# More buffers in the scan, one tile moved, and a replayed instruction order in a two-layer hybrid diffusion step

## The chip, the cores and the metric

One Trainium2 chip, all 8 NeuronCores (two dies of four). Each core runs the same program on its own 1536 tokens, and the metric is device time in microseconds (us) of the slowest core. Some executions fall in a slow state, in which one die (once both) has a lower granted clock and the time is up to 18% longer; those are left out of every ratio. Ratios are the mean time of one kernel's fast runs over the mean of the fast runs of the kernel before in the same rounds on the same chip. The medians that are quoted beside them are those of all runs, slow ones too, so the ratios are not quite the ratios of the medians. A difference of two ratios is turned into time with 2232 us, and then compares kernels that ran in different rounds.

## The reference, cut to what matters

```python
def trunk_layer(x, mods, l, P, init_state, rows):           # twice (DEPTH = 2)
    sh1, sc1, g1, sh2, sc2, g2 = mods
    y, st = token_mixer(x * (1 + sc1) + sh1, l, P, init_state, rows)
    x = layer_norm(ALPHA * x + g1 * y, ...)
    y = swiglu(x * (1 + sc2) + sh2, P['w_gate_up'][l], P['w_down'][l])
    return layer_norm(ALPHA * x + g2 * y, ...), st

def token_mixer(u, l, P, init_state, rows):
    z = u @ P['w_in'][l] + P['b_in'][l]                      # q, k, v, o, gates, Fourier, conv, merge gates
    h, new_state = mlstm_bidir(...)                          # 4 heads of 256, chunks of 128, two directions
    ...                                                      # Fourier mixing, gated short convolution
    merged = sigmoid(gm) * (h_m @ ...) + sigmoid(gf) * (h_f @ ...) + sigmoid(gc) * (h_c @ ...)
    return merged @ P['w_out'][l], new_state
```

The scan (`mlstm_bidir`) goes over chunks in order in both directions. It starts from a cached state C0 for the sample tokens and from zero for the context tokens, and the state after every second chunk is an output.

## The kernel before

The kernel does not write instructions in order. It records operations with their data dependences, and a list scheduler with assumed costs then puts them in an order for each of the five engines. At run time each engine takes its own row strictly in that order and waits on semaphores. In the lines of the profile PE is TensorE, DVE VectorE, ACT ScalarE, POOL GpSimd and SP SyncE, which issues transfers. Buffers are places in SBUF: two tiles that share a place make a dependence between whatever uses them.

The assumed cost of a transfer, in the scheduler:

```python
            if o.kind == "dma":
                s = max(dma_t, t + 1300.0)
                dma_t = s + o.nbytes / dma_rate              # dma_rate = 300 bytes per ns
                o.t1 = dma_t + 700.0
```

The buffers of the scan (kT: keys of a head; ktok: the same, transposed back to tokens; C: states, stored to oC and loaded from C0n; Cb: their bf16 copies; sc: scores; h and hn: outputs of the scan before and after their normalisation):

```python
        kT = R.sb("kT%d" % l, [128, 2, NTOK], BF16, v_p[1].end + 6144)
        ktok = R.sb("ktok%d" % l, [128, NCH, 256], BF16, SG + 4096)
        C_p = Pool(R, "C%d" % l, bv_p.end, [128, 2, 257], F32, 5)
        s_p = Pool(R, "sc%d" % l, ht_p1.end, [128, 512], BF16, 3)
```

One head of the scan:

```python
            for g in range(3):                    # scores and transposed keys, 4 chunks a group
                ...
            for k in range(4):                    # context chunks 8 to 11, both directions
                ...                               # each step: vw on GpSimd, state update on PE, DVE, ACT
            Cc = []
            for d in range(2):
                t = C_p.get()                     # a free state buffer
                R.dma("sp", t[:]..., C0n[l, d, h], ...)
                Cc.append(t)
            for k in range(8):                    # sample chunks 0 to 7, both directions
                ...
        def proj_o(l, h):
            for b in range(3):                    # output gate of the head, by blocks of 512 tokens
                for ec in range(2):
                    pt = proj(oW, ec * 128, 128, b)
                    so = so_p.nxt()
                    R.act(so[:], pt(), AF.Sigmoid, ...)
                    d = hm[h][:, ec, b * 512:(b + 1) * 512]
                    R.tt(d, d, so[:], ALU.mult, n=512, cost=431)
```

The merge stage works with weight tiles r and partial sums ac and mo. It folds Fourier weights (wf) from a staging tile (wst) that lies over buffers of the convolution, and brings x back from memory; in layer 0 GpSimd adds position rows to one block of x:

```python
        ws_p = Pool(R, "wst%d" % l, X + 16 * K1, [128, 4, 2, 128], F32, 1)
        wf_p = Pool(R, "wf%d" % l, ws_p.end, [128, 8, 128], BF16, 2)
        ...
    R.schedule(allowed)
    R.emit_all()
```

## Time and profile before

| | before |
|---|---|
| median of 16 runs, 3 of them slow | 2234.7 us (4 runs when the prediction was made, 1 of them slow: 2235.02) |
| spans of the cores in the profiled run | 2214.7 to 2232.7 us, granted clock 0.987 to 0.992 |
| TensorE (PE) busy, core 6 | 2108.9 us, 94% |
| without a matmul | 123.8 us |

TensorE sets the time, so the profile is read by asking where it stands still. The stages are cut at events: the first state update of a layer begins its scan, the first product of the layer's input u with an r tile ends it, the first product with mg ends the merge, the first gate_up product ends the norm. Length, and the time in it without a matmul, in us, from the timeline and the windows of the slowest core:

| stage | length | idle |
|---|---|---|
| start | 115.5 | 46.8 |
| scan, layer 0 | 255.3 | 24.9 |
| conv and merge, layer 0 | 368.3 | 8.9 |
| norm, FFN and projections between the scans | 469.6 | 6.8 |
| scan, layer 1 | 250.9 | 16.8 |
| conv and merge, layer 1 | 350.7 | 2.3 |
| norm and FFN to the end | 422.5 | 17.2 |

### The profile page before, as it was taken

The page shows a single profiled execution, that of the slowest core. Times are in us where ns is not written, and L with a number is a line of the kernel's source. Part 1 is how long each engine was busy: PE and PEld are TensorE (multiplying, and loading weights), DVE is VectorE, ACT ScalarE, POOL GpSimd, SP SyncE. Part 2 cuts the span into 40 slices and gives each one's busy share as a digit, 9 for nine tenths or more (in the row PEclk, how much of TensorE's full clock was granted, in tenths as well). Part 3 has the DMA queues.
Part 4 walks back from the last instruction along what each step waited for, and adds up shares of the span by engine and source line. Part 5 has one row for each costly group of instructions (what it writes and reads, how often), then busy time and mean ns, then how long its engine had stood idle before and what let it go on. Part 6 is the DMA issues. An engine that isn't in the chain of part 4 may idle for free.

```text
span 2232.7 us, 29934 instructions; the slowest of 8 cores (2214.7 to 2232.7 us)
## 1 busy us (share of the span) xinstructions
PE 2108.9 (94%) x12092; PEld 1092.8 (49%) x12092; DVE 1153.6 (52%) x2229; ACT 872.9 (39%) x1471; POOL 607.7 (27%) x1003
## 2 busy tenths in 40 slices
PE   2898998998999999999999999899999999999997
PEld 1565674443444434444446657544444443444446
DVE  2765775554444772222576667745544469111256
ACT  1466764222222471111355777522222238111124
POOL 1443452113221440011354344311111136000022
PEclk9999999999999999999999999999999999999999
DMA  9634245566443264454035334433533236332212
GB/s 207 137 84 95 72 124 96 104 118 137 81 85 65 83 108 81 90 109 76 38 82 135 77 92 109 105 48 52 132 57 60 41 104 108 57 57 38 53 38 76
DMA packets 73625, 195.97 MB, mean 88 GB/s; under 512 B 7162, under 2 KB 34824, under 8 KB 71824
## 3 DMA queue, kind: packets, MB, share of 16 engines
q0 software_dynamic: 34688, 120.71, 31.7%
q1 hardware_dynamic: 38800, 73.36, 9.6%
q8 instruction: 95, 1.56, 0.3%
q14 instruction: 42, 0.34, 0.1%
HBM read 272.67 MB, written 39.94 MB: 140 GB/s over the span
## 4 chain that ended last, share of the span: by engine, by line
PE 83%; DMA 7%; DVE 6%; ACT 2%; POOL 1%; issue 1%; SPq 0%; DVEq 0%
PE ps L192 82%; DVE x L234 2%; DMA qW<-wpack 2%; DMA oC<-C 1%; DMA wst<-wpack 1%; PE ps L190 1%; DVE C L246 1%; DMA r<-wpack 1%; DMA C<-C0n 1%; DMA x<-xin 1%; ACT x L222 0%; DVE x L246 0%; DVE zsr L234 0%; DMA oW<-wpack 0%; DVE ac L234 0%
## 5 line engine op out<-in xcount | busy, mean ns | idle before, releaser
L192 PE MATMUL ps<-u,r 128*128 128x512 bf16 x2304 | 515.4, 379 | 1.4 <-DVE uc1b L246 0.8
L192 PE MATMUL ps<-u,gu 128*128 128x512 bf16 x2112 | 464.0, 381 | 9.1 <-DVE g L234 7.2
L192 PEld LDWEIGHTS ps<-u,r 128*128 128x128 bf16 x2304 | 222.2, 98 | 268.3 <-issue 2.7
L192 PEld LDWEIGHTS ps<-u,gu 128*128 128x128 bf16 x2112 | 205.2, 98 | 259.6 <-DVE g L234 9.1
L234 DVE TENSOR_TENSOR g<-ps,sa 128x512 bf16<-128x512 f32 x132 | 90.7, 690 | 325.2 <-PE ps L192 325.2
L192 PE MATMUL ps<-g,wd 128*128 128x512 bf16 (+1 forms) x1232 | 230.2, 349 | 0.0
L222 ACT ACTIVATE sa<-ps 128x512 f32<-128x512 f32 x132 | 78.5, 596 | 342.5 <-PE ps L192 342.4
L192 PEld LDWEIGHTS ps<-g,wd 128*128 128x128 bf16 x1232 | 119.8, 98 | 108.4 <-issue 1.0
L222 ACT ACTIVATE sg<-ps,cpk 128x512 f32<-128x512 f32 x102 | 70.0, 686 | 188.2 <-PE ps L192 175.1
L298 POOL DMA_DIRECT2D r<-wpack x112 | 63.1, 564 | 281.0 <-PE ps L192 280.8
L246 DVE SCALAR_TENSOR_TENSOR C<-C,tA__56,ps 128x514 f32<-128x514 f32 x160 | 115.9, 742 | 41.0 <-PE ps L192 33.9
L234 DVE TENSOR_TENSOR x<-x,rn 128x512 f32<-128x512 f32 (+1 forms) x202 | 135.9, 740 | 0.0
L246 DVE SCALAR_TENSOR_TENSOR x<-ps,g1a,x 128x512 f32<-128x512 f32 (+1 forms) x104 | 72.5, 703 | 110.3 <-PE ps L192 109.5
L222 ACT ACTIVATE Cb<-C,tA__56 128x514 bf16<-128x514 f32 x160 | 113.1, 721 | 31.5 <-DVE C L246 17.6
L298 POOL DMA_DIRECT2D gu<-wpack x60 | 32.3, 539 | 313.4 <-PE ps L192 309.4
L258 POOL TENSOR_SCALAR vw<-v,gat 128x257 bf16<-128x257 bf16 x192 | 97.8, 520 | 72.2 <-PE ps L192 64.2
L192 PE MATMUL ps<-u,kW 128*128 128x512 bf16 x384 | 94.6, 394 | 10.9 <-ACT u L222 8.1
L192 PE MATMUL ps<-vW,u 128*128 128x256 bf16 (+1 forms) x768 | 96.2, 277 | 0.0
L192 PE MATMUL ps<-u,oW 128*128 128x512 bf16 x384 | 93.6, 393 | 1.3 <-DMA oW<-wpack 1.1
L192 PE MATMUL ps<-u,qW 128*128 128x512 bf16 x384 | 89.4, 379 | 2.1 <-ACT q L222 1.2
L192 PE MATMUL ps<-hm,r 128*128 128x512 bf16 x384 | 90.9, 379 | 0.0
L192 PE MATMUL ps<-hc,r 128*128 128x512 bf16 x384 | 90.7, 379 | 0.0
(253 smaller groups left out, 2966.1 us busy)
## 6 DMA issues: line engine op xcount, KB each, us to landing
r<-wpack POOLq DMA_DIRECT2D x80, 512.0 KB, 6.3
gu<-wpack POOLq DMA_DIRECT2D x60, 512.0 KB, 6.7
oC<-C SPq DMA_DIRECT2D x96, 256.0 KB, 2.3
wd<-wpack POOLq DMA_DIRECT2D x16, 704.0 KB, 12.5
x<-xin SPq DMA_DIRECT2D x5, 2048.0 KB, 14.5
xspill<-x SPq DMA_DIRECT2D x4, 2048.0 KB, 6.8
r<-wpack POOLq DMA_DIRECT2D x32, 256.0 KB, 6.3
wst<-wpack SPq DMA_DIRECT2D x16, 512.0 KB, 3.8
```

Source lines behind the costliest of these rows:

```text
L190: ins = PE.transpose(out=rap(m[0]), in_=m[1], identity=m[2])
L192: ins = PE.matmul(rap(m[0]), lhsT=m[1], rhs=m[2], start=m[3], stop=m[4])
L222: ins = A.activation(out=rap(out), in_=rap(in_), func=func, **kw)
L234: ins = E.tensor_tensor(out=rap(out), in0=rap(a), in1=rap(b), op=op)
L246: ins = V.scalar_tensor_tensor(out=rap(out), in0=rap(a), scalar=rap(s), in1=rap(b), op0=op0, op1=op1)
L258: ins = E.tensor_scalar(out=rap(out), in0=rap(a), scalar1=s1, scalar2=s2, op0=op0, **kw)
L298: ins = E.dma_start(out=out, in_=in_, **kw)
```

## The change

Its intent: take away waits of TensorE in the scan and at the start of the merge, and let the order be chosen by replaying it against a finer model of the transfers. No computing instruction is added or taken away on any engine; only the number of semaphore instructions differs (29934 instructions in all before, 29916 after). The core of the diff:

```diff
-        kT = R.sb("kT%d" % l, [128, 2, NTOK], BF16, v_p[1].end + 6144)
+        kTs = [R.sb("kT%d_%d" % (l, i), [128, 2, NTOK], BF16, a) for i, a in enumerate((v_p[1].end + 6144, G + 18 * K1))]
...
-        ktok = R.sb("ktok%d" % l, [128, NCH, 256], BF16, SG + 4096)
+        ktoks = [R.sb("ktok%d_%d" % (l, i), [128, NCH, 256], BF16, a) for i, a in enumerate((SG + 4096, G + 12 * K1, SG + 4096, v_p[1].end + 6144))]
...
-        s_p = Pool(R, "sc%d" % l, ht_p1.end, [128, 512], BF16, 3)
+        s_p = Pool(R, "sc%d" % l, ht_p1.end, [128, 512], BF16, 2)
+        for i in range(2):
+            C_p.free.append(R.sb("Cx%d_%d" % (l, i), [128, 2, 257], F32, s_p.end + i * 2080))
...
-            for g in range(3):
+            for g in (2, 0, 1):
...
+            (the two C0 loads moved ahead of the four context steps)
...
-            for b in range(3):
+            for b in (2, 0, 1):                  # in proj_o
...
-        ws_p = Pool(R, "wst%d" % l, X + 16 * K1, [128, 4, 2, 128], F32, 1)
-        wf_p = Pool(R, "wf%d" % l, ws_p.end, [128, 8, 128], BF16, 2)
+        ws_p = Pool(R, "wst%d" % l, X + 28 * K1, [128, 4, 2, 128], F32, 1)
+        wf_p = Pool(R, "wf%d" % l, X + 16 * K1, [128, 8, 128], BF16, 2)
...
-    R.schedule(allowed)
+    R.settle(allowed, 6)        # schedule, replay, feed the replayed transfer times back; best of six
+    (the eight adds of position rows moved apart on GpSimd's row)
```

The v bias tile bv also moves to the front of its region, so that it can be loaded before the second block of x has been used. `settle` and `replay` are some 100 lines that only choose an order.

More of the change, by code (lines that the diff above doesn't have):

```diff
@@ L16 @@
     __slots__ = ("i", "eng", "emit", "deps", "odeps", "cost", "prio", "kind", "tiles", "acc", "nd", "succ",
-                 "est", "t0", "t1", "seqno", "vc", "xdeps", "semkey", "semval", "nbytes", "lead", "tset")
+                 "est", "t0", "t1", "seqno", "vc", "xdeps", "semkey", "semval", "nbytes", "lead", "tset", "row")
 class PT:
@@ L91, in __init__ @@
         self.outputs, self.outkeys = set(), set()
+        self.took, self.log = None, []
         self.fine = set()
@@ L303, in dma @@
         o.lead = chain
+        o.row = 1.0
         if str(out.space) == "DRAM" and out.tensor.name in self.outputs:
@@ L476, in schedule @@
             if o.kind == "dma":
-                s = max(dma_t, t + 1300.0)
-                dma_t = s + o.nbytes / dma_rate
-                o.t1 = dma_t + 700.0
+                if self.took is not None:
+                    o.t1 = t + self.took[o.i]
+                else:
+                    s = max(dma_t, t + 1300.0)
+                    dma_t = s + o.nbytes / dma_rate
+                    o.t1 = dma_t + 700.0
                 fin = o.t1
@@ L505, in schedule, with replay, moving, head @@
         return order
+    def replay(self, seed=None, rate=330.0):
+        import random
+        rng = random.Random(seed)
+        vary = (lambda a, b: rng.uniform(a, b)) if seed is not None else (lambda a, b: 1.0)
+        order = self.order
+        rate *= vary(0.9, 1.05)
+        at = {e: 0 for e in order}
+        free = {e: 0.0 for e in order}
+        end, issued, took = {}, {}, {}
+        queue = {"pool": [], "sp": []}
+        clock, tset = 0.0, None
+        left = len(self.ops)
+        waits = {o: [(d, 0.0 if d.kind == "dma" or d.eng == o.eng else LAT[d.eng]) for d in list(o.deps) + o.xdeps] for o in self.ops}
+        def moving():
+            return [q[0] for q in queue.values() if q and q[0][1] <= clock + 1e-6]
+        ready = {}
+        def head(e):
+            o = order[e][at[e]]
+            t = free[e]
+            for d, lat in waits[o]:
+                x = end.get(d)
+                if x is None:
+                    return None
+                if x + lat > t:
+                    t = x + lat
+            return t
+        while left or queue["pool"] or queue["sp"]:
+            best = None
+            for e in ENGS:
+                if at[e] < len(order[e]):
+                    t = ready.get(e)
+                    if t is None:
+                        t = ready[e] = head(e)
+                    if t is not None and (best is None or t < best[0]):
+                        best = (t, e)
+            mv = moving()
+            nxt = None
+            if mv:
+                total = sum(h[3] for h in mv)
+                nxt = clock + min(h[2] * total / (rate * h[3]) for h in mv)
+            for q in queue.values():
+                if q and q[0][1] > clock + 1e-6 and (nxt is None or q[0][1] < nxt):
+                    nxt = q[0][1]
+            if nxt is not None and (best is None or nxt <= best[0]):
+                t = nxt
+            else:
+                t = max(best[0], clock)
+            for h in mv:
+                h[2] -= (t - clock) * rate * h[3] / total
+            clock = t
+            for n, q in queue.items():
+                if q and q[0][1] <= clock + 1e-6 and q[0][2] <= 1.0:
+                    o = q.pop(0)[0]
+                    end[o] = clock + (700.0 if n == "pool" else 500.0)
+                    took[o.i] = end[o] - issued[o]
+                    if q:
+                        q[0][1] = max(q[0][1], clock)
+            if nxt is not None and (best is None or nxt <= best[0]):
+                continue
+            t, e = best
+            o = order[e][at[e]]
+            at[e] += 1
+            left -= 1
+            ready[e] = None
+            c = o.cost * (1.0 if e == "pe" else vary(0.97, 1.06))
+            if e == "act" and o.tset is not None and o.tset != tset:
+                tset = o.tset
+                c += 1300.0
+            if o.kind == "dma":
+                if e == "pool":
+                    c = 550.0
+                issued[o] = t
+                n = o.nbytes
+                queue[e].append([o, max(t + 1300.0, 4500.0) if e == "pool" else t + 900.0, n * vary(0.97, 1.06), o.row])
+            else:
+                end[o] = t + c
+            free[e] = t + c
+        return max(end.values()), took
@@ L507, in emit_all, with settle @@
+    def settle(self, allowed, tries):
+        best = None
+        for i in range(tries):
+            used = self.took
+            self.schedule(allowed)
+            t, took = self.replay()
+            mean = (t + sum(self.replay(s)[0] for s in range(3))) / 4
+            self.log.append((i, t, mean))
+            if best is None or mean < best[0]:
+                best = (mean, used)
+            self.took = took
+        self.took = best[1]
+        self.schedule(allowed)
     def emit_all(self):
@@ L885, in build_program @@
     un = {"n": 0}
+    PL = []
     def add_places(b, eng="dve", gp=0):
@@ L893, in add_places @@
             z = xb[b][:, k, :].rearrange("p (r q) -> p r q", r=8)
-            R.tt(z, z, a, ALU.add, n=512, eng="pool" if k < gp else eng, cost=None if k < gp or eng == "pool" else 860)
+            o = R.tt(z, z, a, ALU.add, n=512, eng="pool" if k < gp else eng, cost=None if k < gp or eng == "pool" else 860)
+            if eng == "pool":
+                PL.append(o)
     def modulate(b, ks=range(8)):
@@ L1010, in build_program @@
         SG = v_p[0].end + 6144
-        so_p = Pool(R, "so%d" % l, SG, [128, 512], BF16, 4)
-        ktok = R.sb("ktok%d" % l, [128, NCH, 256], BF16, SG + 4096)
+        bv_p = Pool(R, "bv%d" % l, SG, [128, 256], F32, 2)
+        so_p = Pool(R, "so%d" % l, bv_p.end, [128, 512], BF16, 4)
+        SG = bv_p.end
+        ktoks = [R.sb("ktok%d_%d" % (l, i), [128, NCH, 256], BF16, a) for i, a in enumerate((SG + 4096, G + 12 * K1, SG + 4096, v_p[1].end + 6144))]
         hn_p = Pool(R, "hn%d" % l, SG + 4096 + 6144, [128, 2, 256], BF16, 2)
-        bv_p = Pool(R, "bv%d" % l, hn_p.end, [128, 256], F32, 2)
-        C_p = Pool(R, "C%d" % l, bv_p.end, [128, 2, 257], F32, 5)
+        C_p = Pool(R, "C%d" % l, hn_p.end, [128, 2, 257], F32, 5)
         h_p = Pool(R, "h%d" % l, C_p.end, [128, 2, 256], F32, 2)
         ht_p1 = Pool(R, "hta%d" % l, h_p.end, [128, 256], F32, 1)
-        s_p = Pool(R, "sc%d" % l, ht_p1.end, [128, 512], BF16, 3)
-        assert s_p.end <= X + 48 * K1
+        s_p = Pool(R, "sc%d" % l, ht_p1.end, [128, 512], BF16, 2)
+        for i in range(2):
+            C_p.free.append(R.sb("Cx%d_%d" % (l, i), [128, 2, 257], F32, s_p.end + i * 2080))
+        assert s_p.end + 2 * 2080 <= X + 48 * K1
         Cb_p = Pool(R, "Cb%d" % l, R2, [128, 2, 257], BF16, 10)
@@ L1117, in mlstm @@
         def mlstm(l, h):
-            qT, v = q_t[h % 2], v_t[h % 2]
+            qT, v, kT = q_t[h % 2], v_t[h % 2], kTs[h % 2]
             W_ = gat[:, 0, :]
-            STs = []
-            for g in range(3):
+            ktok = ktoks[h]
+            STs = {}
+            for g in (2, 0, 1):
                 ps = PT(R, "T")
@@ L1129, in mlstm @@
                 st = ST_p.nxt()
-                STs.append(st)
+                STs[g] = st
                 sc = s_p.nxt()
@@ L1226, in out_pair @@
                         R.ts(hmv, hv, colp[:, l, j:j + 1], None, ALU.mult, n=256)
+            Cc = []
+            for d in range(2):
+                t = C_p.get()
+                R.dma("sp", t[:].rearrange("p a n -> p (a n)"), C0n[l, d, h], t[:].tensor.name)
+                Cc.append(t)
             Cf = Cbk = None
@@ L1242, in mlstm @@
                     out_pair(8, 11)
-            Cc = []
-            for d in range(2):
-                t = C_p.get()
-                R.dma("sp", t[:].rearrange("p a n -> p (a n)"), C0n[l, d, h], t[:].tensor.name)
-                Cc.append(t)
             for k in range(8):
@@ L1373, in build_program @@
         proj_v(l, 0)
-        evac_q(l, 0, "k", kW, kT)
+        evac_q(l, 0, "k", kW, kTs[0])
         evac_q(l, 0, "q", qW, q_t[0])
@@ L1387, in build_program @@
             if h + 1 < H:
-                evac_q(l, h + 1, "k", kW, kT)
+                evac_q(l, h + 1, "k", kW, kTs[(h + 1) % 2])
                 evac_q(l, h + 1, "q", qW, q_t[(h + 1) % 2])
@@ L1410, in build_program @@
         uc_p.free.append(uc2)
-        assert t1_p.end <= X + 32 * K1
+        assert t1_p.end <= X + 28 * K1
         todo = [(0, t) for t in range(8, 24)] + [(1, t) for t in range(24)] if l == 0 else []
@@ L1467, in build_program @@
         sg_p.free += more.free[2:]
-        assert ac_p.end <= X and more.end <= X + 32 * K1
+        assert ac_p.end <= X and more.end <= X + 28 * K1
         def xback(b):
@@ L1624, in build_program @@
                 R.dma("sp", xs_d[b], flatx(b), "x%d" % b)
-    R.schedule(allowed)
+    R.settle(allowed, 6)
+    q = R.order["pool"]
+    assert len(PL) == 8
+    T = PL[0].t0
+    for o in PL:
+        q.remove(o)
+    for k, o in enumerate(PL):
+        i = next(i for i, p in enumerate(q) if p.t0 > T + 30000.0 + 14000.0 * k)
+        o.t0 = q[i].t0 - 0.5
+        assert q[i - 1].t0 <= o.t0
+        q.insert(i, o)
     R.emit_all()
```

## The prediction

> **What bounds the kernel now.** I read the page first, then the spans of all cores, the waits, the timeline of TensorE around each long wait, and the chain of waits there.
>
> ```profile
> PE 2108.9 (94%) x12092; PEld 1092.8 (49%) x12092; DVE 1153.6 (52%) x2229; ACT 872.9 (39%) x1471; POOL 607.7 (27%) x1003
> ...
> PE 83%; DMA 7%; DVE 6%; ACT 2%; POOL 1%; issue 1%; SPq 0%; DVEq 0%
> ```
>
> TensorE is busy for 2108.9 of 2232.7 us on core 6, the slowest. That leaves 123.8 us without a matmul, and no change of order alone can win much more than that. The cores lie within 18 us of each other (2214.7 to 2232.7), all at a granted clock of 0.987 to 0.992, so the profiled run is undisturbed. The next question is where the 123.8 us lie. Busy time of TensorE by windows, subtracted from each window's length, gives: start (0 to 62) 46.7; first mLSTM stage (130 to 320) 18.4; 320 to 500, its end and the convolution, 7.1; 500 to 620 6.9; the first norm (770 to 840) 5.6; second mLSTM stage (1220 to 1460) 16.8; second norm 5.6; the last 23 us 11.9; the rest 4.8. The waits of TensorE say who ended them (columns: who waited for whom, us in total, times, longest):
>
> ```profile
> PE ps L192 <- DMA adaw<-wpack: 35.8, 8, 17.4
> PE ps L192 <- DVE h L246: 12.1, 8, 7.3
> PE ps L190 <- ACT hn L222: 8.5, 7, 4.1
> PE ps L192 <- ACT u L222: 8.1, 1, 8.1
> PE ps L192 <- DVE C L246: 7.8, 13, 1.2
> ...
> PE ps L192 <- DMA r<-wpack: 6.9, 2, 6.4
> PE ps L192 <- DVE wf L246: 6.8, 1, 6.8
> ```
>
> The first and fourth rows are the start: eight tiles of conditioning weights, then the second third of the activations. The other long ones are single events: 7.25 us ended by h at 194, 6.4 us by a load of r at 364, 6.8 us by wf at 518, and a group of short waits ended by 4.1 us for hn at 1453. The chain of waits over the first and third of these shows that the engine named is only the last link:
>
> ```profile
> 177.16 7.96 DMA oC<-C
> 185.12 0.02 issue
> 185.14 7.40 DMA C<-C0n
> 192.54 0.03 issue
> 192.56 0.72 ACT Cb L222
> ```
>
> ```profile
> 495.19 0.75 DVE uc0b L246
> ...
> 496.37 19.38 DMA wst<-wpack
> 515.77 2.49 DVE wf L246 x2
> ```
>
> In the first, a starting state C could be loaded only when a state buffer was free, that is after the store of an earlier state had landed. In the second, the Fourier weights' staging tile lay over a convolution buffer and could be loaded only after the last convolution (uc0b).
>
> **What the Trainium skill says.** "TensorE: Matmul & The Clock Gate", Part 1 on the HAM clock gate, says that an idle window of about 3.4 us halves the PE's clock and that a busy window of that length restores it. The trace agrees: 16 matmuls of 128x256 took 3.62 us just after the 7.25 us idle, against 1.91 a few us later.
>
> ```profile
> 194.22 0.40 PE L192 MATMUL ps<-vw,ST 128*128 128x257 bf16 x1 [7.25 <-DVE h L246]
> ...
> 195.06 3.62 PE L192 MATMUL ps<-vW,u 128*128 128x256 bf16 x16
> ...
> 201.05 1.91 PE L192 MATMUL ps<-vW,u 128*128 128x256 bf16 x16
> ```
>
> So a long wait costs its idle time and a slow restart that the page counts as busy. "DMA: Bandwidth & Descriptors", section "Issuing engines are not separate DMA queues", says that transfers issued by different engines share the same 16 DMA engines and interleave. The trace agrees: the 512 KB wst load took 19.38 us beside a 2048 KB x load issued 0.4 us before it; its median over the run is 3.8. The same page, section "SWDGE vs HWDGE vs iDMA", says GpSimd builds descriptors in software and SP does not: here 512 KB take 6.3 us from GpSimd (r) against 3.8 from SP (wst).
>
> **The change, part by part.** Counting the instructions of both orders, each engine keeps what it had, in kind and number: nothing is added or removed, only addresses and places in the order change. TensorE's unavoidable work therefore stays; only waits and slow restarts can go.
>
> (1) State buffers go from 5 to 7, one score buffer pays for them, and the loads of C0 move ahead of the four context steps. In the new order of SyncE the two C0 loads of the first head stand before any state store; those of later heads stand before that head's later stores. The 15.4 us of store plus load leave the path. Gain: 7.25 idle, plus the slow restart. Restart: 3.62 - 1.91 = 1.7 for the 16 matmuls, plus about 0.6 for the small ones around it (pairs at 0.64 and 0.58 against 0.39): 2.3. Together 9.5.
>
> (2) The wst tile moves to a place of its own. In the new order it stands ahead of the x load and waits only for a store of the mLSTM stage. Gain: 6.81 idle, plus a slow restart (hfB, 8 matmuls, 2.76 us, and the three after them 1.49; from the warm rates seen elsewhere about 2.0 too much): 8.8.
>
> (3) Loads of r in layer 0. Before, three were issued at 329 to 333 and the fourth only at 356.9, behind GpSimd's late work of the scan; it took 7.36 to land, and TensorE idled 6.37. Now the first four stand together before the end of head 3, and TensorE's order has projections ready after them. Gain: 6.4 idle, plus a restart: the next 13 matmuls took 5.12 us against 13 x 0.226 (16 in 3.62 when warm, the oW projections at 248) = 2.9, so 2.2. Together 8.6. I count 7.5, as another r load may now come late.
>
> (4) The end of head 3 in layer 1. Before, six triples of Cb and vw products, then two transposes of hn stood in a row with nothing between, and two oW projections came last. In the new order the projections and Fourier products lie between these transposes. Gain: the waits from 1441 to 1454 are 1.23 + 0.16 + 1.17 + 0.90 + 4.05 = 7.5; slow matmuls after them (four pairs at 0.64 against 0.39, six oW at 2.77 against 1.4) about 3. Of 10.5 I count 8, as a chain still ends the stage. The same in layer 0 (340 to 360, 2.2 idle): 1.
>
> (5) Two kT and several ktok buffers let head h+1's projections and transposes run earlier, the v projection of block 0 moves into the start, and the order of groups and blocks (2, 0, 1) follows the scan, which starts with chunks 8 to 11. The remaining short waits in the mLSTM stages are 18.4 - 7.25 = 11.1 in layer 0 and 16.8 - 7.5 = 9.3 in layer 1. They are chains over DVE and ACT, each about 0.68 busy there. I count a third: 7. In the start, 128x272 groups fill some of the 8.1 us wait for u, but the last large transfers are as before: 1.
>
> (6) The repeated scheduling with replayed transfers. It only picks the order; its gain is inside the points above. Its formula gives a lone 512 KB load of GpSimd 1.3 + 1.6 + 0.7 = 3.6 us, and the trace has 6.3, so some loads will be placed too late. I take 6 back for new waits.
>
> (7) The eight adds of position rows are moved apart on GpSimd: 9.83 us in one row at 512 become eight of 1.23. No wait of TensorE between 500 and 620 but the one for wf is long, so this frees nothing by itself: 0.
>
> Sum: 9.5 + 8.8 + 7.5 + 8 + 1 + 7 + 1 - 6 = 36.8. I take 35, because parts of two restarts may be counted against waits that other work would have filled. The three undisturbed runs before average (2234.24 + 2235.8 + 2231.15) / 3 = 2233.7; so **2199 us**, a ratio of 0.984.
>
> **Rivals.** First, the scan is bound by its chain over ACT, DVE and GpSimd, and a better filled order only moves the short waits. For it: DVE and ACT at 0.68 in that stage, and thirteen waits for C of at most 1.2 us. Against it: the longest waits there hang on a transfer and on the order at the end of a head. Then only (1), (2) and half of (3) and (4) count, 9.5 + 8.8 + 4 + 4 = 26, minus 6: 2214. Second, new waits take the place of the old: loads planned 2.7 us too short, tiles that now lie over hm (kT of odd heads, ktok of head 1), and fewer score buffers. For it: each row of the order of TensorE is in order, so one late load stops all. Against it: the loads before conv and merge are issued earlier than before in the order. That would leave 10 to 15 us: 2221. Third, all of it works and the chains close up too: the full 38 of points 1 to 4 with their restarts, and half of the 20 of short waits: 48, so 2186. What stays in each case is the start (45), both norms (11) and the end (12).
>
> **Range and chances.** The second rival bounds the range from above and the third from below: 2184 to 2220 should hold it 8 times in 10. Two per cent under 2233.7 is 2189, which needs 44.7 us; of the estimated prize of 38 + 20 + 1 that is three quarters with no new wait. Chances: faster by over 2% 0.2, within 2% 0.79, slower by over 2% 0.01.
>
> **What would show it right or wrong.** Right: no wait for wf, no load of C in the chain of waits, no 6 us wait for r near the end of the first mLSTM stage; in the waits of TensorE, h and hn together (20.6) under 8; TensorE's busy time about 9 us lower through fewer slow restarts; the start, the norms and the end as before. Wrong: a busy time that is unchanged, a new wait of over 3 us for kW, qW, vW, oW or r, or windows of the mLSTM stages with as much idle time as before (35 together). A time at or above 2225 would mean that the reordering gave back what the buffers won; one below 2185 would mean that the short waits were a matter of order and not of the chains.

## The result, and the profile after

| | before | after |
|---|---|---|
| median of all runs | 2234.7 us (16 runs, 13 fast) | 2192.9 us (11 runs, 7 fast) |
| mean of the fast runs | 2233.2 | 2191.8 |
| ratio of fast runs | | 0.9814 (95%: 0.9804 to 0.9825) |
| PE busy, slowest core | 2108.9 | 2097.6 |
| without a matmul | 123.8 | 92.3 |
| spans of the cores | 2214.7 to 2232.7 | 2181.5 to 2189.9 |

The time of the fast runs falls by 41.4 us. The span of the profiled run falls by 42.8: 31.5 of it is idle time and 11.3 busy time, with the same 12092 matmuls (fewer slow restarts). The cores also lie closer together, 8 us in place of 18. The page, and the waits of TensorE on its slowest core, core 1:

```profile
PE 2097.6 (96%) x12092; PEld 1092.1 (50%) x12092; DVE 1156.8 (53%) x2229; ACT 870.8 (40%) x1471; POOL 605.6 (28%) x1003
```

```profile
PE ps L193 <- DMA adaw<-wpack: 35.7, 8, 18.3
PE ps L193 <- DVE g L235: 8.3, 3, 3.2
PE ps L191 <- ACT hn L223: 5.7, 4, 3.5
PE ps L193 <- ACT wp L223: 5.2, 4, 2.5
PE ps L193 <- DMA vW<-wpack: 4.0, 1, 4.0
...
PE ps L193 <- DVE h L247: 2.5, 4, 1.3
```

The waits for wf and r are gone, and those for h have fallen from 12.1 to 2.5. Two of the rows are not what they seem, though. The chain of waits in layer 1, and one row of TensorE's timeline from each layer (start, length, what, and in brackets the idle time before it and what ended it):

```profile
1335.78 7.70 DMA C<-C0n
...
1343.50 0.72 ACT Cb L223
...
1344.95 0.49 ACT hn L223
```

```profile
276.76 1.92 PE L193 MATMUL ps<-wp,ueA 128*128 128x258 bf16 x8 [2.48 <-ACT wp L223]
```

```profile
1345.49 0.40 PE L191 MATMUL ps<-idb,hn 128*128 128x128 bf16 x4 [3.46 <-ACT hn L223]
```

The longest wait for hn (3.46) and the longest for wp (2.48) are both behind a C0 load: ACT stood on a Cb that needed the loaded state, and hn or wp stood behind it in ACT's row. In layer 0 the chain shows the C0 load at 269.06 for 5.92 us, then Cb, then wp. So these loads still reach TensorE, for about 6 us in the two layers together, in place of 7.25 in layer 0 alone plus a longer restart.

By stages (us, slowest core of each run; this table serves all experiments). "To scan 0" is the time from the start to the end of layer 0's scan, "merge 0" the next stage, "layer 1" the projections and the scan of layer 1 together, "rest" everything else.

| kernel | to scan 0 | merge 0 | layer 1 | rest | span |
|---|---|---|---|---|---|
| before | 370.8 | 368.3 | 306.8 | 1186.8 | 2232.7 |
| wst alone | 366.1 | 366.2 | 308.3 | 1187.8 | 2228.4 |
| states and C0 alone | 365.7 | 368.8 | 299.3 | 1185.6 | 2219.4 |
| replay alone | 380.1 | 361.7 | 303.1 | 1187.3 | 2232.2 |
| shuffled order | 365.7 | 369.0 | 299.5 | 1186.4 | 2220.6 |
| kT and ktok alone | 374.5 | 364.4 | 303.3 | 1186.1 | 2228.3 |
| after | 347.8 | 360.9 | 290.9 | 1190.3 | 2189.9 |
| after, scheduled once | 350.4 | 366.1 | 286.8 | 1187.5 | 2190.8 |
| after, adds in one piece | 347.8 | 366.7 | 290.0 | 1187.5 | 2192.0 |
| after, old wst | 345.3 | 364.7 | 292.9 | 1189.7 | 2192.6 |
| after, one kT and ktok | 350.9 | 362.7 | 298.4 | 1187.7 | 2199.7 |
| after, five states, late C0 | 347.5 | 366.7 | 286.3 | 1195.1 | 2195.6 |
| after, slower loads in replay | 344.9 | 369.7 | 294.0 | 1192.0 | 2200.6 |
| after, other replay rate | 353.4 | 359.9 | 291.4 | 1188.8 | 2193.5 |

Of the 42.8 us between the two spans, 23.0 come before the end of layer 0's scan, 7.4 in its merge and 15.9 in layer 1's projections and scan; the rest gives 3.5 back, all of it in layer 1's merge (350.7 to 354.2; its idle time rose from 2.3 to 5.2). The cores of one run differ too: in the kernel before "to scan 0" is 357.0 us on the fastest core and 370.8 on the slowest. The traces of two runs (old wst, one kT and ktok) lack 204 and 201 records of matmuls on their slowest core, so their lengths are used there, and idle time is taken from their cores with all records.

### The profile page after: what moved, and what is told of

The parts are those of the page before. It is cut to its first block, busy times and chain, and to the rows that moved or that the text cites. A ratio compares the mean times of both kernels' runs of the same rounds, so it can differ in the third digit from the quotient of the medians.

```text
span 2189.9 us, 29916 instructions; the slowest of 8 cores (2181.5 to 2189.9 us)
## 1 busy us (share of the span) xinstructions
PE 2097.6 (96%) x12092; PEld 1092.1 (50%) x12092; DVE 1156.8 (53%) x2229; ACT 870.8 (40%) x1471; POOL 605.6 (28%) x1003
## 4 chain that ended last, share of the span: by engine, by line
PE 86%; DVE 6%; DMA 5%; ACT 2%; POOL 1%; issue 0%; DVEq 0%
PE ps L193 85%; DVE x L235 3%; DMA wst<-wpack 2%; DMA adaw<-wpack 1%; PE ps L191 1%; DMA x<-xin 1%; DMA C<-C0n 1%; DVE x L247 0%; ACT x L223 0%; DVE zsr L235 0%; DVE ac L235 0%; DMA cpk<-cpk 0%; POOL u L259 0%; DVE C L247 0%; DVE Cx L247 0%
## 5 line engine op out<-in xcount | busy, mean ns | idle before, releaser
L223 ACT ACTIVATE Cb<-C,tA__56 128x514 bf16<-128x514 f32 x120 | 85.4, 724 | 16.3 <-DVE C L247 8.8
L193 PE MATMUL ps<-mg,r 128*128 128x512 bf16 x384 | 86.3, 379 | 3.9 <-DVE mg L235 3.9
```

The lines of the kernel that those rows point to most:

```text
L193: ins = PE.matmul(rap(m[0]), lhsT=m[1], rhs=m[2], start=m[3], stop=m[4])
L223: ins = A.activation(out=rap(out), in_=rap(in_), func=func, **kw)
```

## The experiments

Twelve kernels ran, all correct. "Alone" means on the kernel before.

### wst alone

```diff
-        ws_p = Pool(R, "wst%d" % l, X + 16 * K1, ...)
-        wf_p = Pool(R, "wf%d" % l, ws_p.end, ...)
+        ws_p = Pool(R, "wst%d" % l, X + 28 * K1, ...)
+        wf_p = Pool(R, "wf%d" % l, X + 16 * K1, ...)
```

> The kernel before with the staging tile wst alone moved to its own place. Theory (the parts add up, point 2 is worth 8.8 us): the 6.8 us wait for wf in layer 0 is gone and the time is about 2225, ratio 0.996 (0.9955 to 0.9970); layer 1 does not change. Rival (the waits move): the wait for wf goes but another one in the merge stage takes its place, ratio above 0.9985.

Measured: 2229.7 us, ratio 0.9992 (0.9978 to 1.0006), 1.8 us, and by the interval not over 5. The first tile was loaded at 353, long before it was needed, and the wait for wf went. Another took its place, as the rival had it (chain of waits, then a row of the waits of TensorE):

```profile
492.84 19.06 DMA wst<-wpack
...
511.93 1.32 DVE wf L246
```

```profile
PE ps L192 <- DVE mo L234: 4.8, 1, 4.8
```

There is one staging tile for eight loads. The load for the second step can go only when the first fold has read the tile, at 492, and by then the 2048 KB load of x (492.06) is ahead of it: it takes 19.06 us again. The change moved the slow load from the first step to the second. That is not the whole cause, though: in the changed kernel the same load is in the chain of waits with 19.39 us (from 474.81), and TensorE then waits for mo for 0.30 us only. What differs is DVE's work behind the load, which here runs beside the eight adds; see the adds in one piece, below.

### States and C0 loads alone

```diff
+            (C0 loads ahead of the context steps)
-        s_p = Pool(R, "sc%d" % l, ht_p1.end, [128, 512], BF16, 3)
+        s_p = Pool(R, "sc%d" % l, ht_p1.end, [128, 512], BF16, 2)
+        (two more state buffers)
```

> The kernel before with only the two more state buffers (one score buffer fewer) and the C0 loads ahead of the context steps. Theory (point 1, 9.5 us): the wait of over 7 us at the first head's C0 load is gone, idle time of TensorE in the two mLSTM stages falls from 35 to about 25 us, time about 2224, ratio 0.9955 (0.993 to 0.997). Rival (chains over ACT and DVE bind there, or one score buffer fewer costs): idle time stays at 32 us or more, ratio above 0.998.

Measured: 2223.2 us, ratio 0.9961 (0.9949 to 0.9973), 8.7 us of 2232. Idle time in the two scans fell from 41.7 to 33.3. The waits in layer 0's scan show what is left there:

```profile
PE ps L192 <- DMA r<-wpack: 4.6, 1, 4.6
PE ps L190 <- ACT hn L222: 4.0, 1, 4.0
...
```

The 7 us wait is gone, the chain of waits of that scan holds no store of a state and no load of C0, and 8.7 is close to the 9.5 predicted. But see the shuffled order below before taking this as proof.

### Replay alone

```diff
-    R.schedule(allowed)
+    R.settle(allowed, 6)
```

> The kernel before with only the replayed, repeated scheduling; buffers and loads untouched. Theory (point 6: it only picks the order, worth little by itself, as the long waits hang on buffers): the waits for the C0 load and for wf stay, ratio 0.995 to 1.002. Rival (the choice of order is what wins, the buffers matter little): ratio 0.990 or less.

Measured: ratio 1.0016 (1.0001 to 1.0031); the median of 2237.7 includes slow runs. The order that the model liked best is, if anything, slower. Layer 0's scan got longer, layer 0's merge shorter. As expected, the wait behind a store of a state and a C0 load stayed in layer 0's scan (6.5 us, ended by q); the one for wf fell to 1.7 us by the order alone.

### Shuffled order

```diff
-    R.schedule(allowed)
+    R.schedule(allowed, 290.0)      # assumed transfer rate, 300 before
```

> The kernel before with the scheduler's assumed transfer rate set from 300 to 290, which means nothing on the chip but shuffles the order. It shows how much a shuffled order alone moves the time. Theory (the waits hang on buffers and chains): within 5 us of before, ratio 0.9975 to 1.0025. Rival (the order is a lottery in which the change drew a good ticket): a shift of 10 us or more in either direction.

Measured: 2222.3 us, ratio 0.9960 (0.9948 to 0.9973). A number that means nothing on the chip moved the time by 9 us, as much as the state buffers did. By stages the two are alike (365.7, 369.0, 299.5 against 365.7, 368.8, 299.3). So the theory that the waits hang on buffers alone fails: the order before was a worse draw than a neighbour of it, and a part worth under about 10 us cannot be read from one time alone. The traces have to say it, and here they do (chain of waits, then TensorE, in layer 0's scan):

```profile
177.57 10.05 DMA oC<-C
...
187.64 5.93 DMA C<-C0n
```

```profile
194.95 3.59 PE L192 MATMUL ps<-vW,u 128*128 128x256 bf16 x16 [5.40 <-ACT q L222]
```

The shuffled order still has the wait behind the store and the C0 load, 5.4 us of it, now under the name of q. What it lost is the wait for r (6.4 us before). With the states alone it is the other way round: the wait behind C0 is gone and 4.6 us for r remain. Two like times, two different sets of waits.

### The change, scheduled once

```diff
-    R.settle(allowed, 6)
+    R.schedule(allowed)
```

> The changed kernel, scheduled once as the kernel before was (no replay, no choice among six); all buffers as changed. What the parts alone gave on the kernel before (0.9992, 0.9961, 1.0016) leaves about 31 of the change's 42 us open. Theory A (the buffers carry it, the replay is a lottery worth under 10 us): ratio 0.979 to 0.986. Theory B (replay and buffers need each other): ratio 0.989 or more.

Measured: 2193.4 us, ratio 0.9824 (0.9809 to 0.9838). The intervals of this and the changed kernel overlap. By the two ratios the replay is worth some 2 us here, which is not clear of nothing; scheduled once, layer 0's merge has two waits for r of 3.7 us together that the changed kernel has not, and layer 1 is 4 us shorter.

### The change, adds in one piece

```diff
-    (the eight adds of position rows moved apart on GpSimd's row)
```

> The changed kernel without the spreading of the eight adds of position rows over GpSimd; TensorE's order is the same instruction for instruction. Theory (point 7, worth nothing by itself): within 2 us of the changed kernel, ratio 0.9805 to 0.9830. Rival (9.8 us of adds in one piece hold up loads of r behind them): a wait of TensorE for r or a sum of over 3 us in the merge stage of layer 0, ratio 0.9835 or more.

Measured: 2195.9 us, ratio 0.9830 (0.9815 to 0.9845). The times of the two are not clear of each other, but here TensorE's row is the same in both kernels, so the traces can be laid on each other. First this kernel's GpSimd and DVE:

```profile
490.01 10.28 POOL L235 TENSOR_TENSOR x<-x,cpk 128x512 f32<-128x512 f32 x8 [5.59 <-DMA x<-xin]
```

```profile
494.17 1.66 DVE L247 SCALAR_TENSOR_TENSOR wf<-wst,cst 128x512 bf16<-128x512 f32 x1 [2.16 <-DMA wst<-wpack]
...
497.43 3.42 DVE L247 SCALAR_TENSOR_TENSOR nn<-tt,cpk,nn 128x512 f32<-128x512 f32 x2
500.88 1.63 DVE L235 TENSOR_TENSOR ac<-nn,mo 128x512 f32<-128x512 f32 x1
502.44 0.68 DVE L235 TENSOR_TENSOR mo<-ps,sg 128x512 f32<-128x512 f32 x1
```

The changed kernel's DVE at the same place, then TensorE in this one:

```profile
494.23 0.75 DVE L247 SCALAR_TENSOR_TENSOR wf<-wst,cst 128x512 bf16<-128x512 f32 x1 [2.29 <-DMA wst<-wpack]
...
495.62 1.41 DVE L247 SCALAR_TENSOR_TENSOR nn<-tt,cpk,nn 128x512 f32<-128x512 f32 x2
497.06 0.69 DVE L235 TENSOR_TENSOR ac<-nn,mo 128x512 f32<-128x512 f32 x1
497.67 0.68 DVE L235 TENSOR_TENSOR mo<-ps,sg 128x512 f32<-128x512 f32 x1
```

```profile
503.17 7.04 PE L193 MATMUL ps<-u,r 128*128 128x512 bf16 x24 [3.59 <-DVE mo L235]
```

In both, DVE starts when wst has landed (494.2) and does the same five instructions (two for wf, two for nn, one for ac) without a pause before it makes mo. Beside GpSimd's adds they take 8.4 us in place of 3.6, each 2.2 to 2.4 times as long; mo comes 4.8 us later, and TensorE waits 3.59 us. (The last of the five, ac, runs beside the add that follows the eight on GpSimd.) That wait is 3.6 us on four cores and 1.1 to 1.9 on the others; in the changed kernel it is 0.4 or less on all. The rival I named (loads of r held up) was not the mechanism, but the cost shows in the trace. The kernel before pays it too: its two folds of wf took 2.48 us beside the adds, against 1.41 in the next run, where the adds are spread.

### The change with the old wst

```diff
-        ws_p = Pool(R, "wst%d" % l, X + 28 * K1, ...)
-        wf_p = Pool(R, "wf%d" % l, X + 16 * K1, ...)
+        ws_p = Pool(R, "wst%d" % l, X + 16 * K1, ...)
+        wf_p = Pool(R, "wf%d" % l, ws_p.end, ...)
```

> The changed kernel with the staging tile wst put back over the convolution's buffer. TensorE's order is nearly the same (88 lines differ). Theory (point 2, 8.8 us): the wait for wf of about 6 us comes back and the ratio is 0.985 to 0.987. Rival (what was seen when it alone was changed: the second load of wst beside x is what binds, so the place of the first hardly matters): under 4 us lost, ratio 0.983 or less.

Measured: 2195.7 us, ratio 0.9834 (0.9819 to 0.9848). In layer 0's merge a wait for wf of 2.6 to 3.3 us came back on four of the eight cores; the other four have none. Before, it was 3.5 to 6.8 on all eight. So the theory fails, and the rival holds in substance: 2.8 us by the medians, 4.5 by the ratios, which overlap with those of the changed kernel. With wst alone this puts the part at 2 to 4.5 us, not 8.8.

### The change with one kT and one ktok

```diff
-        kTs = [... two places ...];  ktoks = [... three places for four heads ...]
+        kTs = [one] * 2;             ktoks = [one] * 4
```

> The changed kernel with one kT and one ktok buffer again; replay, states and wst as changed. Theory A (the second kT and ktok are the largest part, as the other parts alone gave little): ratio 0.987 or more, idle time of TensorE in the mLSTM stages back over 25 us. Theory of the prediction (point 5, at most 7 us): ratio 0.982 to 0.985.

Measured: 2202.0 us, ratio 0.9859 (0.9845 to 0.9874), which lies between what the two theories named. Idle time in the scans is 22.2 to 24.6 us on the six cores with all records (13.2 to 15.2 in the changed kernel), so some 9 us more, and not the 25 that theory A asked for. This is the largest loss of any part left out, with 0.9859 - 0.9814 = 0.0045 of 2232 us, or 10 us. An order alone can cost as much (the slower loads below), so again the time does not prove it and the trace has to. It shows the cause in layer 1 (waits of TensorE, then the chain):

```profile
PE ps L193 <- DVE h L247: 9.5, 4, 8.0
```

```profile
1334.32 9.98 DMA oC<-C
...
1344.36 7.64 DMA C<-C0n
```

The wait for a store and then for C0 is back, though this kernel has seven state buffers and early C0 loads. In layer 0 a C0 load of 9.69 us ends in a wait of 6.3, named hn. Seven buffers do not stop C0 from waiting for a store. That the second kT and ktok give TensorE work of the next head to do meanwhile is the likely reason, but it is not shown: at this place in layer 1 both kernels have Fourier products to fill with, and in the changed kernel the C0 load (1335.78) comes behind a state update and not behind a store.

### The change with five states and late C0 loads

```diff
-        s_p = Pool(R, "sc%d" % l, ht_p1.end, [128, 512], BF16, 2)
-        (two more state buffers)
+        s_p = Pool(R, "sc%d" % l, ht_p1.end, [128, 512], BF16, 3)
-            (C0 loads ahead of the context steps)
+            (C0 loads behind the context steps)
```

> The changed kernel with five state buffers and three score buffers again, and the C0 loads after the context steps. Theory (point 1, 9.5 us): a wait of 5 us or more behind a C0 load comes back in the first mLSTM stage, ratio 0.985 to 0.988. Rival (the second kT gives other work to fill that wait): ratio 0.983 or less.

Measured: 2197.2 us, ratio 0.9833 (0.9819 to 0.9847). No wait of 5 us behind C0 came back in the scan of layer 0, where this is the longest row, nor in that of layer 1. But a wait of 5 us stands at the end of layer 1's last head, on all eight cores, where the changed kernel waits 1.5:

```profile
PE ps L193 <- DVE h L247: 4.3, 6, 1.7
```

```profile
1421.86 0.61 PE L191 MATMUL ps<-idb,hn 128*128 128x128 bf16 x4 [5.04 <-ACT hn L223]
```

No load stands in the chain of this wait: the order has put all oW projections before the last two transposes, and nothing between them. So the second kT can stand in for the state buffers, and here it does. The reverse holds in the kernel with the states alone, but not in the one with one kT and one ktok, where the wait came back with seven buffers: it depends on the order too. The part that was worth 8.7 us alone costs about 4 us, within the lottery, when it is left out, and the 5 us wait could be all of it.

### The change with GpSimd's loads as slow as measured, in the replay

```diff
-    max(t + 1300.0, 4500.0) if e == "pool"
+    max(t + 4000.0, 4500.0) if e == "pool"
```

> The changed kernel with GpSimd's loads taken as 2.7 us slower in the replay, so that a lone 512 KB load takes the 6.3 us that the trace shows. Theory (point 6: new waits come from loads planned too short, up to 6 us): waits of TensorE for loads after the first 60 us fall and the ratio is 0.979 to 0.981. Rival (order lottery): anywhere within 0.978 to 0.986 with no relation to those waits.

Measured: 2204.7 us, ratio 0.9863 (0.9844 to 0.9881). A truer length of the loads gave an order some 11 us slower. The loss is in layer 0's merge (369.7) and layer 1 (294.0), and its longest wait in that merge is 2.6 us for ac, not for a load. So the theory that new waits come from loads planned too short is not borne out. Nor is the loss waiting at all: without a matmul are 92.9 us, as in the changed kernel (92.3), and TensorE's busy time is 2107.7 in place of 2097.6. Its matmuls ran slower, and the record doesn't show why.

### The change with another rate in the replay

```diff
-    def replay(self, seed=None, rate=330.0):
+    def replay(self, seed=None, rate=320.0):
```

> The changed kernel with the replay's assumed rate at 320 in place of 330, which means nothing on the chip: the width of the order lottery on the changed kernel. Theory (with more buffers the order matters less than before, where a like change moved 9 us): within 4 us of the changed kernel, ratio 0.9797 to 0.9832. Rival: 9 us or more away.

Measured: 2196.4 us, ratio 0.9831 (0.9817 to 0.9845), 3.8 us slower, just inside what the theory allowed. With the slower loads, though, the lottery on the changed kernel spans some 11 us, so it is no narrower than before. But the four orders tried of the whole change (this one, slower loads, scheduled once, the changed kernel) lie between 0.9814 and 0.9863, and the five kernels made from the one before between 0.996 and 1.002. The lottery is too small to account for the change.

### kT and ktok alone

On the kernel before:

```diff
-        kT = R.sb("kT%d" % l, ...)
+        kTs = [... two places ...]
-        ktok = R.sb("ktok%d" % l, ...)
+        ktoks = [... three places for four heads ...]
```

> The kernel before with only the second kT and the ktok buffers; five state buffers, late C0 loads, old wst, old order of groups, one scheduling. Theory (the second kT and ktok let the next head's projections and score products fill whatever wait the scan has, the one behind the C0 load too, which is why leaving single parts out of the changed kernel cost little): both mLSTM stages, 506 us before and 468 after, shorten by 20 us or more, waits of TensorE of 5 us or more vanish from them, ratio 0.986 to 0.992. Rival (the buffers only pay together with the state buffers and the order of groups): the stages shorten by under 12 us, the wait behind the C0 load stays, ratio 0.994 or more.

Measured: 2230.0 us, ratio 0.9985 (0.9972 to 0.9998). By time the rival held: to the end of scan 0 it took 374.5, longer than before. The wait behind the C0 load did not simply stay, though: in layer 0 a C0 load of 11.21 us is in the chain and TensorE waits 2.5 us at most around it, while in layer 1 one of 5.61 us behind a store of 8.84 ends in a wait of 4.5. What is missing shows at the end of head 3 in layer 1. This kernel, then the changed one:

```profile
1449.82 0.61 PE L190 MATMUL ps<-idb,hn 128*128 128x128 bf16 x4 [4.21 <-ACT hn L222]
1450.22 4.73 PE L192 MATMUL ps<-u,oW 128*128 128x512 bf16 x16
```

```profile
1409.14 0.39 PE L191 MATMUL ps<-idb,hn 128*128 128x128 bf16 x4
...
1410.22 1.89 PE L193 MATMUL ps<-u,oW 128*128 128x512 bf16 x8
...
1415.59 0.40 PE L191 MATMUL ps<-idb,hn 128*128 128x128 bf16 x4 [1.53 <-ACT hn L223]
```

With the blocks of proj_o in the order 0, 1, 2, the last two oW projections (16 matmuls) come in one piece after the last transposes of hn, when TensorE has just waited for them. This is so at the end of layer 1's scan in all six kernels with the old order, which wait 2.6 to 5.1 us there. In the changed kernel they stand between the transposes. In all eight kernels with the new order they come before the last transposes, and seven of these wait 1.5 to 2.2 us; the eighth is the one with late C0 loads, with 5.04. So the order of blocks goes with this wait, but does not settle it. By the code, block 2 (chunks 8 to 11) is the one that the scan finishes first.

## Why the prediction was right

The total was 35 us and came out at 41.4; the range held it. The mechanism (no work removed, waits of TensorE in the scan and in layer 0's merge closed, slow restarts gone with them, start, norms and end unchanged) is what the traces show: busy time fell by 11.3 against 9 predicted, the start from 46.8 to 44.8 us idle, and the FFN stages did not move. That the sum came so near is partly luck: points 1, 2 and 7 were off one way or the other, and what the parts gave alone is a quarter of the whole. Three of the signs that I named went against me: C0 loads are still in the chain of waits, h and hn together are 8.2 us and not under 8, and the start has a new wait of 4.0 us for vW, over the 3 that I had called a sign of being wrong. The steps fared as follows.

**Point 1, state buffers, 9.5 us.** Right alone (8.7), though a shuffled order gave as much. In the changed kernel it is hardly needed: left out, it costs about 4, within the lottery. "No load of C in the chain of waits" was wrong: C0 loads still end waits of 2.48 and 3.46 us, disguised as wp and hn. I took the number of buffers for the cure, and the kernel with one kT shows the same store and load with seven of them.

**Point 2, wst, 8.8 us.** Mis-sized: 1.8 alone, 3 to 4.5 left out. I followed the first load and did not ask what the next of eight loads into the one tile would meet. It meets the same x, and DVE's work behind it meets the adds of point 7, so the two points belong together. I had also read the wait on core 6 alone, where it is 6.8 us; over the eight cores it is 3.5 to 6.8.

**Points 3 and 4, r and the end of head 3, 7.5 and 9 us.** The waits went as predicted, and in the traces both go with the order, not with one part. The 6.4 us wait for r is gone already from wst alone and from the shuffled order, and one of 3.2 us is in the kernel with late C0 loads. The wait for hn at the end of layer 1 is 2.6 us or more in each kernel with the old order of blocks in proj_o, but 5.0 in one with the new order. The slow matmuls that I put at about 3 in point 4 sum to 2.4 (1.0 and 1.4).

**Point 5, kT, ktok and the order of groups, 7 us.** The step that was sized too low. kT and ktok alone are worth 3.4 us, yet 10 us when left out of the whole, as far as the lottery lets one say. And the four parts that were run alone add up to 1.8 + 8.7 + 3.4 - 3.6 = 10.3 us of 41.4. The other 31 must then lie in what they do together, in the order of groups and blocks, in the place of bv and in the draw of the order; order of groups and blocks, bv and the spread adds were not run alone.

**Point 6, 6 us for new waits.** Some came (2.48 and 3.46 behind C0, and 4.0 for vW in the start, which stands for part of the 8.1 us for u before), but not for the reason given: correcting the length of loads made the kernel slower.

**Point 7, the adds, nothing.** Wrong: the trace with the adds in one piece shows a wait of up to 3.6 us that the spreading avoids. I looked for a wait of TensorE that ended with GpSimd and found none. But the adds act through DVE, whose instructions took over twice as long beside them; the line in the prediction, 2.49 us for two folds of wf, already showed it.

One reading of the prediction was wrong, although nothing hangs on it. The slow wst load (19.38 us, its median over the run 3.8) was set down as agreeing with what "DMA: Bandwidth & Descriptors" says of transfers from different engines. Both wst and x are issued by SyncE, 0.40 us apart; x took 15.9 us and wst landed 3.9 us after it. No run here was made to show two engines' transfers side by side.

The first rival (the chains bind, the longest waits stay filled only where a transfer was at fault, 2214) and the second (new waits take it back, 2221) are refuted by the time, though waits did move as the second had it (wst alone). The third (short waits close too, 2186) is as near to the result as my own figure (6 us from each): idle time in the two scans fell from 41.7 to 15.2.

What stays open: how much of the 31 us is the order of groups in the scores, how much the order of blocks in proj_o, how much bv, how much wst and the adds together. Stage lengths point to them: to the end of scan 0, every kernel with all three took 344.9 to 353.4 us, every one without them 365.7 to 380.1, whatever else it had (over all cores, 340.5 to 353.4 and 355.6 to 380.1). That is a correlation over fourteen kernels, not an experiment. Every kernel of the first group also had at least three of the four other parts.

## What to carry to other kernels

Where a scheduler sets the order, first measure what an irrelevant constant does to the time; here it was 9 us, and no single part of that size can be judged by its time alone. Judge it by the wait that it removes, whatever name the wait goes by, by what stands next in line for the same tile, queue or engine, and by what runs beside it. Buffers that let other work fill a wait and buffers that shorten it can stand in for each other: measured alone and left out they give different answers, and the sum of the parts (10 us here) need not be near the whole (42).

## What the Trainium skill lacked or had wrong

- "TensorE: Matmul & The Clock Gate" (Part 1, the warning on the peak-current limiter) tells one to budget 13/16 of the clock for dense matmuls on all cores. With TensorE 94 to 96% busy the cores of all fast runs were granted 0.985 to 0.997. Clocks near the page's figure were seen in slow runs alone: one die was granted between 0.82 (2580 us, the changed kernel) and 0.97 in them. For this kernel the measurement decides.
- The same page, same part, gives an idle window of about 3.4 us for the slow clock, and of shorter idles between matmuls it says that they can do the same, without a size. Here is one: before, in layer 1's head 3, waits of 1.23, 0.16 and 1.17 us with short work between them (2.56 us idle in 3.35) were followed by matmul pairs of 0.64 us in place of 0.39; after, a wait of 2.48 us, with 1.32 us three us earlier, was followed by eight matmuls of 1.92 us, against 1.06 for the same form when warm.
- "DMA: Bandwidth & Descriptors" has no figure for what a load loses behind a larger one that the same engine issued just before. Here a 512 KB load of 3.8 us median took 19.1 to 19.4 us when SyncE had issued a 2048 KB load 0.4 to 0.8 us before it; in the kernel before it landed 3.9 us after that load.
